# The gate's sixteen modulation tiles by quarters inside the up projection, and a transformer block's end in a written order

## The chip, the cores and the metric

The kernel runs on one core of one Trainium2 chip. The metric is the device time of one execution in microseconds (us), the median of several runs; lower is better. The core has five engines with a queue of their own, which run side by side and wait for each other through semaphores: TensorE (PE, matmuls), VectorE (DVE), ScalarE (ACT), GpSimd (POOL) and SyncE (SP, which here only issues transfers). Every instruction of one engine runs in the order of that engine's queue. Transfers (DMA) move data between the device memory and the on-chip memory.

## The reference

One block of a diffusion transformer over 512 latent tokens, with 256 context tokens beside them; the model width is 2048, the feed-forward width 5504, all in 32-bit floats. What matters for the change:

```python
mod_l = (jax.nn.silu(c) @ w_ada[l] + b_ada[l])[:, None, :]
sh_a, sc_a, gt_a, sh_f, sc_f, gt_f = jnp.split(mod_l, 6, axis=-1)
...
x = x + gt_a * merge_heads(att_l, conv_l, g_mix_out[l], w_out[l])
...
hf_l = modulate(rms_norm(x, g_ffn_norm[l]), sh_f, sc_f)
x = x + gt_f * conv_ffn(hf_l, w_up[l], ffn_conv_w[l], ffn_conv_b[l], w_down[l])
return rms_norm(x, g_final)
```

`mod_l` has 6 x 2048 = 96 x 128 values. The kernel keeps them as 96 columns of 128 (a *modulation tile* each): 32 to 47 are `gt_a`, 48 to 63 `sh_f`, 64 to 79 `sc_f`, and 80 to 95 `gt_f`, the gate of the feed-forward part, which is first needed when the down projection's second sum is scaled.

## The kernel before

**Precision.** A matmul in 32-bit precision is made of three (`mm3`, lines 183 to 185): each operand is split into a high and a low part, and high x high, high x low and low x high are summed. For a weight tile ACT writes the high part (a CAST, line 984) and DVE the low part (line 985). So for every product PE waits for ACT first, and one matmul later for DVE.

**Stages.** The input projection runs to 430 us of the profiled execution, the attention to 625, the output projection to 808. There the residual, the norm of its result and the modulated input `hf` of the feed-forward part are made. The up projection begins with plain rows (tiles `uf`, weights `ufw0`, `ufw1`, ...). From 880 to 1680 us it runs over f = 3 to 42 by seven products per f, in the manner of Strassen and Winograd: `p1`, `p2`, `p6`, `q5`, `p7`, and one f later `q4` and `q3`. A product (`product`, line 1151) is 24 matmuls of 128 x 256. Its operands are four weight tiles and sums of them: of the loads `11`, `12`, `s1`, `s3` and `22` that SP issues (line 1105), `s1` and `s3` are added to in memory by a POOL transfer (line 1107), then DVE computes a11 += s1 (line 1199) and a12 += a11 (line 1200). The five tiles take their place in a ring of nine buffers, so a load of f+2 starts when a product of f is done with its tile. The down projection follows: 7 plain rows to 1782 us, then 24 steps v0 to v23 of the same seven products, with 18 matmuls each, to 2141 us. Its results are the tiles c0 to c15 (`into`, line 1312). Step v22 yields c12 and c13, v23 c14 and c15.

**Modulation tiles.** A tile is a dot product of a row block of `w_ada` with silu(c): a load of 128 x 2048 values and DVE's multiply-and-sum. Tiles 32 to 87 are done in the output projection, in halves of 1024 (`late_dot`, line 247, DVE line 251, tiles `ada`). Tiles 88 to 95 are done by quarters of 512 (`gate_mods`, line 1227, DVE line 1234, tiles `aq`) in the plain rows of the down projection.

**Between the projections.** The last two tiles of the output projection are computed in halves of 256 tokens (`ol`). For the first half, then for the second, DVE adds the residual (line 943, tiles `x14`, `x15`), ACT squares it, DVE adds the squares up (line 335, `fq0t`), PE sums over partitions (line 300), ACT takes the root (line 277, with a table load), DVE the reciprocal (line 279, `rr`), PE spreads it over the partitions (line 284), and `hf_tile` (line 919) multiplies, scales and splits each tile (`x0`, `hf0h`, `hf0l`, ...).

**The end.** The final norm goes by halves of 256 tokens too. `scale_out` (line 1390) scales c tiles by the gain on ACT into `out` tiles (line 1393), `final` (line 1381) multiplies by the reciprocal root on DVE (line 1386) and issues the stores (line 1387). The last two steps and the end are written out from line 1437 on.

**Order.** The program order is written by hand only in part: a scheduler with a cost table of its own reorders each engine's instructions ahead of the run. `keep` fixes an instruction's place among those kept, `tc.issue_after` sets one behind another, and generators (`pump`, `next(gm)`) deal out side work between products: `pump(1)` takes one step of the list `bg`, which holds above all the pair sums of the convolution (`pair_sums`, tiles `ts`, `tp`).

## Time and profile before

| | |
|---|---|
| median of 3 runs | 2158.14 us |
| the three runs | 2158.14, 2150.28, 2158.75 us |
| the profiled execution | 2158.0 us |
| its span (first to last instruction) | 2156.2 us |
| outside of the span | 1.8 us |
| mean granted TensorE clock | 0.992 |
| idle time of PE in the span | 2156.2 - 2104.1 = 52.1 us |

The span is what the views of the profile divide up. A busy PE is not always at its peak: the profile gives beside the busy time the clock that was granted, 1.00 being full. The views used below are the page's table of engines, the windows (a row for a stretch: its length, each engine's busy time with its instructions, the granted clock, the share of time in which the transfer engines were busy, and GB/s), the list of what PE waited for (tile and line that waited, the releaser, total us, times, and longest), and the timeline (start in us, duration in us, engine, line, operation, output <- inputs, and in brackets the idle time ahead with what ended it). The timeline leaves the buffers' numbers out of the names: `v` is any of a step's weight tiles, `v23s` its `s1` or `s3`, `u_s` those of the up projection, `c` any c tile.

### The profile page before, as it was taken

Reading aid. Unit: us, or ns where it says so; the run is one execution under the profiler, and the core shown is the slowest. Engines: PE = TensorE matmul, PEld = TensorE weight load, DVE = VectorE, ACT = ScalarE, POOL = GpSimd, SP = SyncE. Lnnn points to the kernel's source line nnn. Section 1 sums busy time; section 2 is a strip of 40 time slices with the busy share of each in tenths; the row PEclk is TensorE's granted clock in tenths of the full one; section 3 lists DMA queues with packets and bytes.
Section 4 is the critical chain, followed back from the end, with each engine's and each line's share of the span. In section 5 each row is a group of like instructions: output and inputs, shape, how many; then the busy total and the mean of one; then the engine's idle time right before and its main releaser. Section 6 shows DMA issues by size and latency. Waiting matters only on the chain.

```text
span 2156.2 us, 37750 instructions
## 1 busy us (share of the span) xinstructions
PE 2104.1 (98%) x14458; PEld 1946.8 (90%) x14458; DVE 1770.6 (82%) x2859; ACT 1046.8 (49%) x1709; POOL 188.1 (9%) x270
## 2 busy tenths in 40 slices
PE   7999999999999999999999999999999999999996
PEld 4788788888988888999999999999999889999996
DVE  7998987778886989788888888788888659888886
ACT  5533333555542237555555555555555333333445
POOL 0000000000000000111111111111111000000000
PEclk9999999999999999999999999999999999999998
DMA  9989885334559986677877877887877998877773
GB/s 338 348 274 334 268 284 177 130 125 157 181 198 345 357 272 187 160 216 201 242 230 215 239 225 223 239 235 214 238 229 219 345 331 289 260 217 235 210 234 110
DMA packets 162409, 513.89 MB, mean 238 GB/s; under 512 B 18994, under 2 KB 23346, under 8 KB 156594
## 3 DMA queue, kind: packets, MB, share of 16 engines
q1 hardware_dynamic: 132564, 417.10, 56.7%
q0 software_dynamic: 27488, 92.29, 18.2%
q8 instruction: 113, 1.85, 0.3%
q10 hardware_dynamic: 2176, 2.10, 0.3%
q14 instruction: 68, 0.56, 0.1%
HBM read 464.22 MB, written 46.14 MB: 237 GB/s over the span
## 4 chain that ended last, share of the span: by engine, by line
PE 90%; DVE 4%; DMA 3%; ACT 2%; issue 1%; SPq 0%; DVEq 0%; ACTq 0%
PE pp L183 4%; PE pp L185 4%; PE pp L184 4%; PE o L183 1%; PE o L184 1%; PE o L185 1%; PE d L183 1%; PE d L185 1%; PE d L184 1%; PE uf L183 1%; DMA ada<-in_w_ada 1%; PE uf L184 1%; PE uf L185 1%; PE of L183 1%; PE of L184 1%; PE of L185 1%
## 5 line engine op out<-in xcount | busy, mean ns | idle before, releaser
L1030 POOL DMA_DIRECT2D t_d<-tp x126 | 71.8, 573 | 469.1 <-DVE tp L1029 466.7
L251 DVE SCALAR_TENSOR_TENSOR ada<-ada,sv 128x1024 f32<-128x1024 f32 x68 | 82.1, 1220 | 13.5 <-DMA ada<-in_w_ada 13.5
L166 ACT CAST w_0h<-rw 128x512 fp32r<-128x512 f32 (+1 forms) x63 | 38.3, 618 | 106.2 <-PE pp L184 65.4
L1107 POOL DMA_DIRECT2D u_s<-in_w_up x80 | 70.2, 877 | 225.2 <-DMA u_s<-in_w_up 109.8
L229 DVE SCALAR_TENSOR_TENSOR ada<-ada,sv 128x1024 f32<-128x1024 f32 x64 | 77.6, 1219 | 3.8 <-DMA ada<-in_w_ada 3.6
L510 DVE SCALAR_TENSOR_TENSOR ada<-ada,svc 128x1024 f32<-128x1024 f32 x64 | 76.0, 1220 | 2.8 <-DMA ada<-in_w_ada 2.8
L1028 ACT CAST tp<-a 128x256 fp32r<-128x256 f32 x90 | 34.7, 404 | 63.2 <-DMA t_d<-tp 51.8
L773 POOL TENSOR_TENSOR gr<-gr,half 128x8 f32<-128x8 f32 x4 | 10.1, 2522 | 627.8 <-DVE gr L772 535.8
L167 DVE TENSOR_TENSOR w_0l<-rw,w_0h 128x512 fp32r<-128x512 f32 (+1 forms) x63 | 42.6, 682 | 21.7 <-ACT w_0h L166 21.7
L251 DVE SCALAR_TENSOR_TENSOR ra<-ra,sv 128x1024 f32<-128x1024 f32 x44 | 52.5, 1219 | 1.4 <-DMA ra<-in_w_ada 1.3
L1199 DVE TENSOR_TENSOR u<-u,u_s 128x1024 f32<-128x1024 f32 x40 | 48.8, 1220 | 1.1 <-DMA u_s<-in_w_up 1.0
L1200 DVE TENSOR_TENSOR u<-u,u 128x1024 f32<-128x1024 f32 x40 | 48.7, 1218 | 0.0
L1029 DVE TENSOR_TENSOR tp<-a,tp 128x256 fp32r<-128x256 f32 x90 | 36.2, 418 | 13.8 <-ACT tp L1028 13.7
L744 ACT CAST pth<-t 128x384 fp32r<-128x384 f32 x64 | 28.6, 485 | 26.5 <-PE t L741 26.5
L521 DVE TENSOR_TENSOR acc<-acc,pp 128x512 f32<-128x512 f32 x50 | 34.0, 681 | 2.1 <-PE pp L185 2.1
L745 DVE TENSOR_TENSOR ptl<-t,pth 128x384 fp32r<-128x384 f32 x64 | 33.3, 550 | 2.7 <-ACT pth L744 2.7
L1028 ACT CAST tp<-ts 128x256 fp32r<-128x256 f32 x36 | 14.6, 407 | 41.5 <-DMA t_d<-tp 39.6
L725 DVE TENSOR_REDUCE mn<-s 128x1 f32<-128x768 f32 x32 | 30.4, 953 | 4.7 <-PE s L714 4.6
L1029 DVE TENSOR_TENSOR tp<-ts,tp 128x256 fp32r<-128x256 f32 x36 | 15.2, 422 | 22.3 <-ACT tp L1028 22.3
L991 ACT ACTIVATE g<-cg,sm 128x512 f32<-128x512 f32 x40 | 32.5, 813 | 0.6 <-DVE cg L1168 0.6
L991 ACT ACTIVATE a<-ca,sm 128x512 f32<-128x512 f32 x40 | 32.1, 803 | 0.0
L999 ACT ACTIVATE g<-g 128x512 f32<-128x512 f32 x43 | 27.1, 631 | 6.4 <-DVE g L993 6.4
(15965 smaller groups left out, 9401.3 us busy)
## 6 DMA issues: line engine op xcount, KB each, us to landing
ada<-in_w_ada SPq DMA_DIRECT2D x196, 512.0 KB, 6.0
u<-in_w_up SPq DMA_DIRECT2D x120, 512.0 KB, 8.3
w<-t_d SPq DMA_DIRECT2D x161, 256.0 KB, 5.3
u_s<-in_w_up SPq DMA_DIRECT2D x80, 512.0 KB, 4.2
u_s<-in_w_up POOLq DMA_DIRECT2D x80, 512.0 KB, 9.1
t_d<-tp POOLq DMA_DIRECT2D x126, 256.0 KB, 4.9
v<-in_w_dnw SPq DMA_DIRECT2D x72, 384.0 KB, 5.4
ra<-in_w_ada SPq DMA_DIRECT2D x22, 1024.0 KB, 4.9
```

Of the source, the lines that this page charges most:

```text
L183: PE.matmul(ps, w[0], x[0], start=first, stop=False, skip_group_check=on_top)
L184: PE.matmul(ps, w[0], x[1], start=False, stop=False, skip_group_check=on_top)
L185: PE.matmul(ps, w[1], x[0], start=False, stop=last, skip_group_check=on_top)
L229: V.scalar_tensor_tensor(out=r, in0=r, scalar=1.0, in1=vec[:, i * 1024:(i + 1) * 1024], op0=ALU.mult, op1=ALU.mult, accum_out=col[:, i:i + 1])
L251: keep(V.scalar_tensor_tensor(out=r, in0=r, scalar=1.0, in1=svs[i], op0=ALU.mult, op1=ALU.mult, accum_out=lc[:, t % 4:t % 4 + 1] if i else ...
L510: keep(V.scalar_tensor_tensor(out=raw[q], in0=raw[q], scalar=1.0, in1=svc[:, q * 1024:(q + 1) * 1024], op0=ALU.mult, op1=ALU.mult, accum_o ...
L991: A.activation(u, src, AF.Identity, bias=s("fb", m), scale=s("fw", 86 + m))
L1028: A.copy(out=z[:, :256], in_=src)
L1029: V.tensor_tensor(out=z[:, 256:], in0=src, in1=z[:, :256].bitcast(F32), op=ALU.subtract)
L1030: G_.dma_start(t_d[p, OPS.index(n)], z.bitcast(F32))
L1107: G_.dma_start(r[-1], src[more], accum_op=ALU.add)
L1199: V.tensor_tensor(out=a11, in0=a11, in1=s1, op=ALU.add)
```

## The change

It has four parts.

1. Of the tiles 80 to 95, eight leave the output projection (`late["end"]` goes from 88 to 80) and eight leave the plain rows of the down projection. All sixteen are now done as 64 quarters inside the up projection's products: `between` takes a step of `bg`, or, when `bg` is empty, the next quarter. A quarter is one 256 KB load into the single buffer `ts`, which the pair sums use too, and one DVE multiply-and-sum of 128 x 512; the next load can start when that buffer is free.
2. The tiles `12` and `s3` of the last step get buffers of their own rather than two of the ring.
3. The first matmuls behind a norm's sums and behind its spread are issued after them (`hold`, `behind`), at the end of the down projection.
4. The end's order is written out: the table for the root is loaded ahead by a small root of its own, `pump` sits inside products, the c tiles' last sums and the output products are kept in the order written, and the first half's stores are all issued by SP.

```diff
-    late = {"t": 32, "raw": None, "end": 88}
+    late = {"t": 32, "raw": None, "end": 80}
...
     def mm3(ps, w, x, first, last, on_top=False):
-        PE.matmul(ps, w[0], x[0], start=first, stop=False, skip_group_check=on_top)
+        with tc.issue_after(behind.pop()) if behind else ExitStack():
+            PE.matmul(ps, w[0], x[0], start=first, stop=False, skip_group_check=on_top)
...
+    def gate_mods():
+
+        for q in range(4):
+            SP.dma_start(rl, sv_d[:, q * T:(q + 1) * T])
+            for i in range(16):
+                r = cp.tile([P, T], F32, tag="ts", bufs=1, name=f"aq{i}{q}")
+                SP.dma_start(r, w_ada[80 + i][:, q * T:(q + 1) * T])
+                yield
+                V.scalar_tensor_tensor(out=r, in0=r, scalar=1.0, in1=rl, op0=ALU.mult, op1=ALU.mult, accum_out=parts[q // 2][:, i, q % 2:q % 2 + 1])
...
+    def between():
+
+        if bg:
+            pump(1)
+        else:
+            next(gm, None)
+
     def product(ps, a, n, nm, first):
...
-        pump(1)
+        between()
...
-        z.a11, z.s1, z.a12, z.s3, z.a22 = (raw4(f"v{st}{x}")[:, :n] for x in ("11", "s1", "12", "s3", "22"))
+        own = ("12", "s3") if st == STEPS - 1 else ()
+        z.a11, z.s1, z.a12, z.s3, z.a22 = ((dp.tile([P, 2 * T], F32, tag="sq", bufs=2, name=f"v{st}{x}") if x in own else raw4(f"v{st}{x}"))[:, :n] for x in ("11", "s1", "12", "s3", "22"))
...
-            (A if j % 4 else SP).dma_start(out[j:j + 2, :, HS[h]].rearrange("a p t -> p a t"), o)
+            (A if h and j % 4 else SP).dma_start(out[j:j + 2, :, HS[h]].rearrange("a p t -> p a t"), o)
...
-    bg.append(rms_steps(sqs, D, 0, T // 2, rl, wait=1, one=True))
+    bg.append(rms_steps(sqs, D, 0, T // 2, rl, wait=1, one=True, hold=True))
     outs = final(0, rl[:, HS[0]], scaled)
-    d_q5(za)
+    with tc.issue_after(last_hi[0]):
+        A.activation(tiny(1, "root"), eps, AF.Sqrt)
+    pump(1)
+    d_q5(za, (3,))
     squares(za.m + 1, H1)
-    pump(2)
-    d_q5(zb)
+    d_q5(zb, (1,), lambda: [keep(next(outs)) for _ in range(2)])
+    keep(last_into[0])
     squares(zb.m + 1, H1)
-    pump(1)
     scaled = {j: scale_out(j, 1) for j in range(0, za.m, 2)}
-    for _ in range(3):
-        next(outs)
+    keep(next(outs))
     d_q3(za)
+    keep(last_into[0])
     sqs = [ssq, add_squares(None, acc2[za.m][:, H1], T // 2, "eqc", a=T // 2)]
-    for _ in range(3):
-        next(outs)
+    for _ in range(2):
+        keep(next(outs))
     d_q3(zb)
+    keep(last_into[0])
+    for _ in range(2):
+        keep(next(outs))
     sqs.append(add_squares(None, acc2[zb.m][:, H1], T // 2, "eqd", a=T // 2))
     *_, r = rms_steps(sqs, D, T // 2, T // 2, None, one=True)
+    keep(recips[0])
     for ins in outs:
         keep(ins)
```

How this moves the instructions shows at three places. The first is DVE's queue at the end of the output projection; `x14` and `x15` are the last two residual tiles by halves, `fq0t` the sum of squares, `ada86` and `ada87` modulation tiles. Before:

```order
L251 SCALAR_TENSOR_TENSOR ada860_7370,mod_90<-ada860_7370,sv_93 128x1024
L943 SCALAR_TENSOR_TENSOR x14_7265<-ol0_7263,mod_90,x14_7265 128x256
L251 SCALAR_TENSOR_TENSOR ada861_7372,lc_94<-ada861_7372,sv_93 128x1024
L251 SCALAR_TENSOR_TENSOR ada870_7408,mod_90<-ada870_7408,sv_93 128x1024
L335 TENSOR_TENSOR fq0t_6497<-fq0t_6497,fq14_7508 128x256
L279 RECIPROCAL rr_7488<-rr_7488 128x2
L251 SCALAR_TENSOR_TENSOR ada871_7410,lc_94<-ada871_7410,sv_93 128x1024
L256 TENSOR_TENSOR mod_90<-mod_90,lc_94 128x4
L257 TENSOR_TENSOR mod_90<-mod_90,sm_82 128x4
L943 SCALAR_TENSOR_TENSOR x15_7267<-ol1_7264,mod_90,x15_7267 128x256
```

And now:

```order
L283 RECIPROCAL rr_7436<-rr_7436 128x2
L955 SCALAR_TENSOR_TENSOR x14_7243<-ol0_7241,mod_90,x14_7243 128x256
L347 TENSOR_TENSOR fq0t_6497<-fq0t_6497,fq14_7456 128x256
L938 TENSOR_TENSOR x0_6494<-x0_6494,rl_92 128x256
L938 TENSOR_TENSOR x1_6500<-x1_6500,rl_92 128x256
...
L942 TENSOR_TENSOR hf0l_7496<-x0_6494,hf0h_7495 128x256
L938 TENSOR_TENSOR x2_6507<-x2_6507,rl_92 128x256
L942 TENSOR_TENSOR hf1l_7520<-x1_6500,hf1h_7519 128x256
L938 TENSOR_TENSOR x3_6514<-x3_6514,rl_92 128x256
L274 SCALAR_TENSOR_TENSOR fs4_7876<-mod_90,sm_82 128x1
L955 SCALAR_TENSOR_TENSOR x15_7245<-ol1_7242,mod_90,x15_7245 128x256
```

The dots ahead of the last residual are gone, the reciprocal of the first half stands ahead of `x14`, and the first `hf` tiles are made ahead of `x15`.

The second place is the up projection. SP's queue, around the loads of f = 13 and 14 (`aq101` is quarter 1 of tile 80 + 10):

```order
L1119 DMA u13_11_10613<-in_w_up 128x1024
L1119 DMA u13_12_10615<-in_w_up 128x1024
L1175 DMA aq101_10430<-in_w_ada 128x512
L1175 DMA aq111_10464<-in_w_ada 128x512
L1119 DMA u13_s1_10617<-in_w_up 128x1024
L1119 DMA u13_s3_10620<-in_w_up 128x1024
L1175 DMA aq121_10496<-in_w_ada 128x512
L1119 DMA u13_22_10623<-in_w_up 128x1024
L1119 DMA u14_11_10872<-in_w_up 128x1024
```

Before, the same loads of `11`, `12`, `s1`, `s3`, `22` followed one another with nothing between them. The quarters' loads now stand ahead of `s1` and between `s3` and `22`, each waiting for the one buffer `ts`. On DVE the multiply-and-sum of `aq101` stands between a12 += a11 of f = 12 and the low part `u11q4l`, that of `aq111` behind `u11q3l`, and that of `aq121` ahead of `u12p7l`; quarters are found so up to f = 28.

The third place is DVE's queue in the last two steps. Before, from the second product of v22 on:

```order
L985 TENSOR_TENSOR v22p2l_23364<-v2212_23131,v22p2h_23363 128x768
...
L985 TENSOR_TENSOR v22p6l_23465<-v2211_23129,v22p6h_23464 128x768
L1319 SCALAR_TENSOR_TENSOR c14_19136<-v23a_23413,mod_90,c14_19136 128x256
L1273 TENSOR_TENSOR v23s3_23329<-v2311_23326,v23s1_23327 128x768
...
L985 TENSOR_TENSOR v21q3l_23488<-v2112_22934,v21q3h_23487 128x768
L1319 SCALAR_TENSOR_TENSOR c12_19132<-v22a_23337,mod_90,c12_19132 128x256
L1329 TENSOR_TENSOR v2311_23326<-v2311_23326,v23s1_23327 128x768
L1330 TENSOR_TENSOR v2312_23328<-v2312_23328,v2311_23326 128x768
```

And now:

```order
L999 TENSOR_TENSOR v22p2l_23405<-v2212_23172,v22p2h_23404 128x768
L1296 TENSOR_TENSOR v23s3_23370<-v2311_23367,v23s1_23368 128x768
...
L999 TENSOR_TENSOR v23p2l_23481<-v2312_23369,v23p2h_23480 128x768
L1342 SCALAR_TENSOR_TENSOR c12_19187<-v22b_23379,mod_90,c12_19187 128x256
L1355 TENSOR_TENSOR v2311_23367<-v2311_23367,v23s1_23368 128x768
L1342 SCALAR_TENSOR_TENSOR c11_19185<-v21a_23181,gn_95,c11_19185 128x256
L999 TENSOR_TENSOR v22p6l_23506<-v2211_23170,v22p6h_23505 128x768
L1356 TENSOR_TENSOR v2312_23369<-v2312_23369,v2311_23367 128x768
```

The sum `s3` = a11 + s1 of v23, behind which POOL adds to `s1` in memory, now stands right behind `v22p2l`, and a11 += s1, which needs that addition, six rows ahead of `v21q3l` rather than two behind it. On ACT the high part `v23p6h`, made from that a11, stands behind 11 output scalings rather than 15, counted from `v21q3h`.

More of the change, by code (lines that the diff above doesn't have):

```diff
@@ L299, in rms_steps @@
             for g in range(ng):
-                PE.matmul(ps[:, g:g + 1], sq[:, a + g * P:a + (g + 1) * P], ones[:, 0:1], start=i == 0 and g == 0, stop=i == len(sqs) - 1 and g == ng - 1)
+                ins = PE.matmul(ps[:, g:g + 1], sq[:, a + g * P:a + (g + 1) * P], ones[:, 0:1], start=i == 0 and g == 0, stop=i == len(sqs) - 1 and g == ng - 1)
+        if hold:
+            behind.append(ins.ins)
         r = tiny(4, "rr")[:, :ng]
@@ L304, in rms_steps @@
             yield
-        spread(pb, r)
+        ins = spread(pb, r)
+        if hold:
+            behind.append(ins)
         if dst is not None:
@@ L1214, in block_kernel @@
     finish(pend)
+    assert next(gm, None) is None
     phc.close()
@@ L1290, in block_kernel @@
             pump(1)
-            for _ in range(2):
-                next(gm, None)
             for _ in range(2 if h == 0 else 3):
@@ L1410, in block_kernel @@
         d_q5(z)
-        next(gm, None)
         if first:
```

60 lines of the change are left out of this document (29 added, 31 removed).

## The prediction

> **What bounds the kernel now.** The page's table of engines comes first, then windows over the long stages.
>
> ```profile
> span 2156.2 us, 37750 instructions
> PE 2104.1 (98%) x14458; PEld 1946.8 (90%) x14458; DVE 1770.6 (82%) x2859; ACT 1046.8 (49%) x1709; POOL 188.1 (9%) x270
> ...
> 625.00:808.00 183.00, 183.00 (x886) 152.97 (x885) 150.01 (x275) 56.73 (x99) 11.97 (x18) 0.99 0.90 324
> 880.00:1680.00 800.00, 800.00 (x6653) 799.25 (x6653) 663.27 (x877) 461.52 (x689) 139.62 (x208) 1.00 0.79 224
> 1680.00:1782.00 102.00, 100.99 (x529) 86.00 (x528) 60.19 (x115) 36.64 (x53) 6.05 (x10) 1.00 0.96 343
> ```
>
> PE is busy for 2104.1 of 2156.2 us, and in the output projection (625 to 808) and the up projection (880 to 1680) it has no idle time. The clock there is 0.99 to 1.00. So work taken from DVE or the transfers inside those stages gains nothing; only PE's few gaps can. The list of PE's waits says where those are:
>
> ```profile
> PE v23a L183 <- ACT v23p6h L984: 3.6, 1, 3.6
> PE rs L300 <- DVE fq0t L335: 3.0, 1, 3.0
> PE rs L300 <- ACT eqdt L331: 2.2, 1, 2.2
> ```
>
> The change touches three of these places: the boundary (`fq0t`, `ufw0h`), the last two steps (`v23p6h`) and the end (`eqdt`). The windows there also show a lower clock:
>
> ```profile
> 810.00:815.00 5.00, 2.48 (x13) 2.40 (x13) 4.50 (x14) 4.38 (x10) 0.54 (x1) 0.74 0.99 322
> 815.00:820.00 5.00, 5.00 (x28) 5.00 (x28) 4.47 (x11) 4.32 (x11) 0.00 (x0) 0.58 1.03 413
> 820.00:825.00 5.00, 5.00 (x45) 5.00 (x44) 4.69 (x16) 4.09 (x12) 0.00 (x0) 1.00 0.97 383
> 2095.00:2100.00 5.00, 4.27 (x36) 4.06 (x35) 4.26 (x7) 2.61 (x4) 0.00 (x0) 1.00 0.40 157
> 2120.00:2125.00 5.00, 5.00 (x32) 5.00 (x32) 3.48 (x7) 2.72 (x5) 0.00 (x0) 0.69 0.00 0
> ```
>
> Behind each of the two long gaps PE is busy without a break, but at 0.58 and 0.69 of its clock: 28 and 32 instructions in 5 us, where 45 fit at a full clock in the row from 820. That is (45 - 28) x 0.111 = 1.9 us lost in 815 to 820 alone, and with the parts of the neighbouring slices some 2.8 us behind each gap. A gap costs its length and then this.
>
> **The change, part by part.** *The boundary.* The timeline of before:
>
> ```profile
> 807.80 0.28 PE L185 MATMUL ol<-mx15h,o151w1536l 128*128 128x256 f32 x1
> 808.56 1.23 DVE L251 SCALAR_TENSOR_TENSOR ada<-ada,sv 128x1024 f32<-128x1024 f32 x1 [0.36 <-DMA ada<-in_w_ada]
> 810.11 0.48 DVE L943 SCALAR_TENSOR_TENSOR x<-ol,mod,x 128x256 f32<-128x256 f32 x1
> 811.17 0.42 DVE L335 TENSOR_TENSOR fq0t<-fq0t,fq 128x256 f32<-128x256 f32 x1
> 811.64 0.61 PE L300 MATMUL rs<-io,fq0t 128*128 128x1 f32 x4 [2.96 <-DVE fq0t L335]
> 812.25 0.83 ACT L984 CAST ufw0h<-ufr 128x768 fp32r<-128x768 f32 x1
> 813.13 0.58 PE L183 MATMUL uf<-hf0h,ufw0h 128*128 128x256 f32 x1 [0.88 <-ACT ufw0h L984]
> ```
>
> PE's last dense matmul ends at 808.08. The residual that follows from it (810.11) stands behind a dot (808.56) that waited for its load, and starts 2.0 us late. Without the dots: the residual from about 808.2 (0.48), the square 0.4, the sum 0.42, and PE's sums at about 809.7. ACT, meanwhile, has one scaling of 0.4 and then `ufw0h` (0.83) behind the square, so the plain rows start at about 809.2 + 0.4 + 0.4 + 0.83 + 0.1 = 811.0 rather than 813.13: **2.1 us** gained. At worst ten DVE operations that now stand ahead of `x15` are late by as much (0); at best the restart follows PE's sums at once, 2.1 + 0.8 = 2.9. Whether the lower clock stays is taken up below.
>
> *The last two steps.*
>
> ```profile
> 2097.01 0.95 DVE L985 TENSOR_TENSOR v22p2l<-v,v22p2h 128x768 fp32r<-128x768 f32 x1
> ...
> 2103.55 0.48 DVE L1319 SCALAR_TENSOR_TENSOR c<-v21a,gn,c 128x256 f32<-128x256 f32 x1 [0.60 <-PE v21a L185]
> ...
> 2104.63 0.84 ACT L984 CAST v23p2h<-v 128x768 fp32r<-128x768 f32 x1 [4.89 <-DMA v<-in_w_dnw]
> 2109.12 0.85 POOL L1274 DMA_DIRECT2D v23s<-in_w_dnw  x1 [20.20 <-DVE v23s L1273]
> 2110.04 6.09 ACT L1393 ACTIVATE out<-c,sm 128x256 f32<-128x256 f32 x15
> 2114.19 0.96 DVE L1329 TENSOR_TENSOR v<-v,v23s 128x768 f32<-128x768 f32 x1 [2.67 <-DMA v23s<-in_w_dnw]
> 2116.91 0.58 PE L183 MATMUL v23a<-w,v23p6h 128*128 128x256 f32 x1 [3.57 <-ACT v23p6h L984]
> ```
>
> The chain is: `s3` on DVE, POOL's addition into `s1`, which lands 2114.19 - 2109.97 = 4.2 us after POOL is done, a11 += s1, and `v23p6h` on ACT behind 15 scalings of 6.09 / 15 = 0.41 us. Now `s3` follows `v22p2l` (2097.01), so POOL's addition can be issued near 2100 and land at about 2104, and ACT becomes the last. Its wait of 4.89 us for `v23p2h`'s load goes, since that load now has a buffer of its own; the next high part then starts when PE frees its buffer, behind the product that ended at about 2103.4 (the row of 2103.55), where it started at 2104.63 + 0.74 = 2105.4. The rest of ACT's queue comes 1.9 earlier with it: the scalings from 2108.1, 11 of them 4.5, `v23p6h` 0.8: ready at 2113.4. PE's products ahead of it, which ended 3.6 before 2116.9 at 2113.3, lose smaller waits and end at about 2112. PE restarts at 2113.5 and waits once more, 0.8, for the low part: in effect 2114.4 rather than 2116.9, less 0.3, because the `s3` put in ahead pushes back `v21q4l`: **2.2 us** gained. With no second wait it is 3.0. If POOL's addition takes 9.2 us to land, as in the up projection (1289.91 to 1299.08, below), a11 += s1 comes at 2109 and holds up the low part of `v22p6` behind it by 3, and 0.5 or so is left.
>
> *The clock behind the gaps.* The gaps were 813.13 - 808.08 = 5.1 and 3.6 us, and are now about 2.9 (with PE's small sums in between) and 1.6 + 0.8. In 2095 to 2100 PE was idle for 0.73 at a clock of 1.00. So the trace bounds the limit: a gap of 0.7 keeps the clock, one of 3.6 loses it. Mine lie in between; the shorter, split one is nearer to the lower end. I take it that the tail's 2.8 us are won and the boundary's are not: **2.8 us**, between 0 and 5.6. [...]
>
> *The end.*
>
> ```profile
> 2139.26 3.69 DVE L1386 TENSOR_TENSOR out<-out,rl 128x512 f32<-128x512 f32 x6
> 2142.87 0.48 DVE L1319 SCALAR_TENSOR_TENSOR c<-v23c,mod,c 128x256 f32<-128x256 f32 x1
> 2145.36 1.27 DVE L1386 TENSOR_TENSOR out<-out,rl 128x512 f32<-128x512 f32 x2
> ```
>
> The last sum into c14 (2142.87) stands behind six output products of 3.69 / 6 = 0.61 us. Now two products, a sum of squares and one product stand there, with two of the six put behind: from 2139.3 that is 2 x 0.61 + 0.42 + 0.61 = 2141.5, 1.4 earlier, and PE's wait of 2.2 for `eqdt`, the square of c14, falls by as much. Between the reciprocal and the second half's products stands one product, not two: 0.6 earlier. **2.0 us**, from 0 (the spread of the root ends last) to 3.0 (the five saved products in full).
>
> *The up projection* takes the 64 quarters. Their cost on DVE is in the rows of before, and so is what stands near it:
>
> ```profile
> L1234 DVE SCALAR_TENSOR_TENSOR aq<-aq,svq x32: 683/687/693, 1703.2 to 1788.1; 128x512 f32<-128x512 f32 x32
> ...
> 1285.55 3.60 SPq L1105 DMA_DIRECT2D u_s<-in_w_up  x2
> ...
> 1289.91 0.89 POOL L1107 DMA_DIRECT2D u_s<-in_w_up  x1 [1.23 <-DMA u_s<-in_w_up]
> ...
> 1299.08 1.23 DVE L1199 TENSOR_TENSOR u<-u,u_s 128x1024 f32<-128x1024 f32 x1 [0.18 <-DMA u_s<-in_w_up]
> 1300.82 1.22 DVE L985 TENSOR_TENSOR u24p2l<-u,u24p2h 128x1024 fp32r<-128x1024 f32 x1
> 1303.76 1.22 DVE L985 TENSOR_TENSOR u23q4l<-u,u23q4h 128x1024 fp32r<-128x1024 f32 x1
> 1304.48 0.29 PE L185 MATMUL u24b<-hf1h,u24p2l 128*128 128x256 f32 x1
> ...
> 1305.01 2.47 SPq L1105 DMA_DIRECT2D u_s<-in_w_up  x2
> ...
> 1299.00:1301.00 2.00, 2.00 (x19) 2.00 (x18) 1.93 (x3) 0.62 (x1) 0.00 (x0) 1.00 1.06 274
> 1303.00:1305.00 2.00, 2.00 (x19) 2.00 (x18) 2.00 (x3) 1.23 (x4) 0.00 (x0) 1.00 0.04 14
> ```
>
> 64 x 0.69 = 44 us of DVE go beside 800 - 663 = 137 us of idle DVE. But there is a loop: `u23q4l` ends at 1304.98 and frees the buffer for the next `s1` load (issued 1305.01; the one before 1285.55); load 4.4, POOL's addition 9.2, then a11 += s1, `p2l` and `q4l` again, 5.9: 19.5 us, against PE's 20 us per f. PE needs `u24p2l`, ready at 1302.04, at 1304.48: 2.4 us in hand. A quarter's load is 256 KB, at the 274 GB/s of a full stretch 0.95 us; one in three falls into the idle transfers of 1303 to 1305 (0.04), the others share with load and addition. With some three quarters in an f the loop grows to 19.5 + 0.5 to 1.2; a dot ahead of `q4l` (0.6) stands where a piece of the convolution (0.4 to 0.7) stood. That is 20.0 to 20.7, over 22 f with quarters and less the 2.4 in hand: 0 to 13 us lost. Nearest to the row with 0.18 of waiting is the low end; I take **1.5 us**.
>
> *The down projection's start* loses 32 dots and loads. PE has 101.0 of 102 us there: at most 1.0, taken as 0. The same holds for the output projection (183.00 of 183). The table load on ACT and the stores moved to SP cost nothing beside a waiting PE.
>
> **The sum**, against the profiled execution (2158.0, which is 0.1 under the median): 2158.0 - 2.1 - 2.2 - 2.8 - 2.0 + 1.5 = **2150.4 us**.
>
> **The rivals.** *Both gaps keep the clock*: 2.8 more, 2147.6. For it: the boundary's new gap is broken by PE's sums. Against: 2.9 is close to the 3.6 that lost it. [...] *Neither does*: 2153.2. *The quarters eat the gain*: the loop at 20.3 gives 22 x 0.3 = 7 less 2.4 in hand, and further waits of a quarter for its own load, up to about 6 in all; 2155 to 2158, no change. *Slower*: the loop at 21.2 us or more, when two quarters of 0.95 each prolong both load and addition in full and a dot adds 0.6 to DVE's part. Each f then takes the loop's time: 22 x 1.2 - 2.4 = 24, and 2150.4 - 1.5 + 24 = 2173. It decides from a loop of 20.5 (22 x 0.5 - 2.4 = 8.6, all of the gain). For it: transfers are full from 1290 to 1301, the loop lacks only 0.5, and the single buffer lets no load run ahead. [...] Against: 4 us in each f are all but idle, and a loop that lags starts its loads into a longer idle stretch.
>
> **How the numbers follow.** The forecast has 0.35, both clocks 0.21, neither 0.14, gain eaten 0.20, slower 0.10. Within 0.5% of 2158.1, about what a measurement of this kernel can tell from no change, is 2147.3 to 2168.9. Faster: half of *both clocks* and a little of the forecast with the upper bounds of boundary and end, 0.18. Slower: 0.09. Same: 0.73. The range runs from 2144 (both clocks and 3.6 of the bounds) to 2160; what lies beyond is most of *slower* and a tenth of the fast side.
>
> **What would show it.** The first plain row at about 811 and the slices 810 to 820 (still below 1.00); `v23p6h` awaited for under 2 us and 2110 to 2125 at a full clock; c14 behind one output product. PE in 880 to 1680 must stay at 20.0 us per f with no wait; the row to look at is a11 += s1 and its wait for `u_s`. The forecast is wrong if that wait exceeds 2 us in many f.

## The result, and the profile after

The changed kernel takes 2262.67 us (median of 4 runs, 2257.75 to 2265.75), the kernel before beside it 2158.44 (4 runs, 2150.28 to 2161.53): a ratio of **1.048 [1.046, 1.051]**. It is slower by 104 us, where 8 us faster was forecast, and outside the range of 2144 to 2160.

The head of the profile's page, its table of engines and the chain that ended last:

```profile
span 2262.9 us, 37775 instructions
PE 2136.8 (94%) x14458; PEld 1969.9 (87%) x14458; DVE 1772.3 (78%) x2888; ACT 1046.0 (46%) x1710; POOL 187.8 (8%) x270
...
PE 60%; DMA 21%; DVE 10%; issue 4%; ACT 3%; POOL 1%; DVEq 0%; SPq 0%; POOLq 0%; ACTq 0%
```

The work is what it was: DVE is busy 1.7 us longer than before, ACT 0.8 less. What is new are 126.1 us in which PE stands, 52.1 before, and a chain that leaves PE for transfers and DVE in 31 of 100 parts, 7 before. The windows say where (columns as before the prediction: length; busy us and instructions of PE, PEld, DVE, ACT, POOL; granted clock; transfer share; GB/s):

```profile
880.00:1280.00 400.00, 373.12 (x3002) 368.86 (x3002) 316.27 (x453) 202.04 (x290) 53.46 (x77) 0.97 0.77 219
1280.00:1680.00 400.00, 353.69 (x2784) 349.38 (x2783) 295.59 (x434) 194.54 (x303) 68.96 (x105) 0.94 0.73 210
```

The up projection, without a gap before, has 73 us of idle PE in these 800, and behind the gaps a clock of 0.97 and 0.94. The transfers are not busier than before (0.77 and 0.73), and DVE and ACT are less so. So no engine is the bound: they wait for each other. From the end of f = 3 to the end of f = 42 (the last matmul of `p7`, read from the timeline) the stage takes 897.4 us against 786.0: **111.4 us**, more than the whole loss. PE stands for 77.1 us of it; the other 34 go with the lower clock behind the gaps, so a gap costs its length and then more, as the prediction has it for the boundary. The list of waits (who waited, line, for whom: total us, times, longest us):

```profile
PE u24a L187 <- ACT u24p1h L998: 7.4, 1, 7.4
PE u31a L187 <- ACT u31p1h L998: 5.2, 1, 5.2
...
PE u7a L189 <- DVE u7p1l L999: 3.9, 1, 3.9
...
DVE tp L1043 <- ACT tp L1042: 84.5, 34, 7.9
DVE aq L1177 <- DMA aq<-in_w_ada: 71.0, 30, 6.6
...
DVE u L1242 <- DMA u_s<-in_w_up: 4.8, 3, 2.7
...
ACT tp L1042 <- DMA t_d<-tp: 142.5, 47, 10.2
```

PE waits for high parts that ACT makes late (47 of the 77 us, 35 of them at `p1h`) and for low parts that DVE makes late (30, of them 18 at `p1l`). DVE waits 71 us for quarters' own loads; the row that was to be watched, a11 += s1 for `u_s`, has 4.8. And ACT waits up to 10.2 us at a cast of the pair sums (`tp`) for the store of an earlier `tp` tile. Of before the same row reads:

```profile
ACT tp L1028 <- DMA t_d<-tp: 91.4, 59, 3.5
```

So ACT always waited there, often, and it cost PE nothing; what is new is the longest. The timeline around PE's wait of 7.4 us (start, duration, engine; in brackets the idle time ahead and what ended it):

```profile
1338.41 1.03 ACT L998 CAST u23p7h<-u_s 128x1024 fp32r<-128x1024 f32 x1
1338.43 0.84 POOL L1121 DMA_DIRECT2D u_s<-in_w_up  x1 [0.78 <-DMA u_s<-in_w_up]
1338.97 0.87 POOL L1044 DMA_DIRECT2D t_d<-tp  x1
1340.77 0.58 POOL L1044 DMA_DIRECT2D t_d<-tp  x1 [0.93 <-DVE a L1007]
...
1349.66 0.40 ACT L1042 CAST tp<-a 128x256 fp32r<-128x256 f32 x1 [10.22 <-DMA t_d<-tp]
1349.98 1.04 ACT L998 CAST u24p1h<-u 128x1024 fp32r<-128x1024 f32 x1
1350.10 0.42 DVE L1043 TENSOR_TENSOR tp<-a,tp 128x256 fp32r<-128x256 f32 x1 [7.92 <-ACT tp L1042]
1351.07 0.58 PE L187 MATMUL u24a<-hf0h,u24p1h 128*128 128x256 f32 x1 [7.43 <-ACT u24p1h L998]
```

ACT stands at a `tp` cast for a store to land. Behind it in ACT's queue stands `u24p1h`, which waited for nothing itself; DVE stands at the cast's other half, and PE at `u24p1h`. Two such casts had run at 1335.09 and 1335.55, and the third, next of the sums, finds its tile still held by a store, which POOL issued at 1338.97 and which took 10.7 us to land. A landing of that length is nothing new: the 126 stores took 4.9 us in the median and 11.7 at the longest before, 5.1 and 12.0 after. New is where the casts that wait for them stand. Counted in the trace, three casts start within 4 us 11 times after the change, twice before it.

The order of the program shows why they come in clumps. DVE's queue at f = 10 to 12, `ts1` and `tp1..` being pair 1 of the sums; before the change, then after (rows left out at "..."):

```
L985 TENSOR_TENSOR u11p2l<-u11_12,u11p2h 128x1024
L1034 TENSOR_TENSOR ts1<-a9 128x256
L985 TENSOR_TENSOR u10q4l<-u10_22,u10q4h 128x1024
...
L985 TENSOR_TENSOR u12p2l<-u12_12,u12p2h 128x1024
L1042 SCALAR_TENSOR_TENSOR ts1<-ts1,a10 128x256
```

```
L1043 TENSOR_TENSOR tp111<-a9,tp111 128x256
L999 TENSOR_TENSOR u10q3l<-u10_12,u10q3h 128x1024
L1177 SCALAR_TENSOR_TENSOR aq81,modc_91<-aq81,rl_92 128x512
...
L1177 SCALAR_TENSOR_TENSOR aq121,modc_91<-aq121,rl_92 128x512
L999 TENSOR_TENSOR u12p7l<-u12_s3,u12p7h 128x1024
L1048 TENSOR_TENSOR ts1<-a9 128x256
L1056 SCALAR_TENSOR_TENSOR ts1<-ts1,a10 128x256
```

The two steps of `ts1` were seven products apart; now the single buffer goes to five quarters first; the first step comes twelve products later than it did, the second five, and both together. At f = 24 the sums are at pair 5 where they were at 7; they make it up in a hurry until f = 36. So 38 of the 111 us are lost in f = 29 to 42, behind the last quarter (at 1452.6 us, in f = 28).

### The profile page after: what moved, and what is told of

Its sections match the earlier page's. It is cut to its first block, busy times and chain, and to the rows that moved or that the text cites. A ratio compares the mean times of both kernels' runs of the same rounds, so it can differ in the third digit from the quotient of the medians.

```text
span 2262.9 us, 37775 instructions
## 1 busy us (share of the span) xinstructions
PE 2136.8 (94%) x14458; PEld 1969.9 (87%) x14458; DVE 1772.3 (78%) x2888; ACT 1046.0 (46%) x1710; POOL 187.8 (8%) x270
## 4 chain that ended last, share of the span: by engine, by line
PE 60%; DMA 21%; DVE 10%; issue 4%; ACT 3%; POOL 1%; DVEq 0%; SPq 0%; POOLq 0%; ACTq 0%
DMA t_d<-tp 7%; DMA aq<-in_w_ada 7%; DMA u_s<-in_w_up 4%; PE pp L187 4%; PE pp L189 4%; PE pp L188 4%; PE o L187 1%; PE o L189 1%; PE o L188 1%; DMA ada<-in_w_ada 1%; PE d L187 1%; PE d L188 1%; PE d L189 1%; PE of L187 1%; PE of L188 1%
## 5 line engine op out<-in xcount | busy, mean ns | idle before, releaser
L1044 POOL DMA_DIRECT2D t_d<-tp x126 | 77.4, 631 | 433.7 <-DVE tp L1043 410.2
L1177 DVE SCALAR_TENSOR_TENSOR aq<-aq,rl 128x512 f32<-128x512 f32 x64 | 44.1, 688 | 71.2 <-DMA aq<-in_w_ada 71.0
L233 DVE SCALAR_TENSOR_TENSOR ada<-ada,sv 128x1024 f32<-128x1024 f32 x64 | 77.6, 1219 | 3.9 <-DMA ada<-in_w_ada 3.7
L255 DVE SCALAR_TENSOR_TENSOR ada<-ada,sv 128x1024 f32<-128x1024 f32 x52 | 62.7, 1219 | 8.0 <-DMA ada<-in_w_ada 7.9
L1042 ACT CAST tp<-ts 128x256 fp32r<-128x256 f32 x36 | 14.6, 405 | 58.7 <-DMA t_d<-tp 38.9
L1005 ACT ACTIVATE g<-cg,sm 128x512 f32<-128x512 f32 x40 | 32.6, 814 | 7.6 <-DVE cg L1211 5.4
```

Source lines behind the costliest of these rows:

```text
L233: V.scalar_tensor_tensor(out=r, in0=r, scalar=1.0, in1=vec[:, i * 1024:(i + 1) * 1024], op0=ALU.mult, op1=ALU.mult, accum_out=col[:, i:i + 1])
L255: keep(V.scalar_tensor_tensor(out=r, in0=r, scalar=1.0, in1=svs[i], op0=ALU.mult, op1=ALU.mult, accum_out=lc[:, t % 4:t % 4 + 1] if i else ...
L1042: A.copy(out=z[:, :256], in_=src)
L1044: G_.dma_start(t_d[p, OPS.index(n)], z.bitcast(F32))
```

## The experiments

Suspected were: the buffer `ts` that quarters and pair sums share (theory A); a dot in DVE's queue that waits for its own load (B); the transfers themselves, on the loop of the `s1` loads (C, the prediction's rival); the dots as such, which take DVE's time and put other work late in the queues (D); and a special form of that (E): a cast of the sums right ahead of `p1h`. "Stretch" is the time from the end of `p7` of f = 3 to that of f = 42 in the profiled run, "idle" the part of it in which PE stands. Each ratio is to the kernel before as it ran beside that kernel (medians 2156.84 to 2160.20). Where PE has no gap the stretch repeats: 786.0 us in four kernels, and 785.2 in e1.

| kernel | median us | ratio [95%] | stretch | idle |
|---|---|---|---|---|
| before | 2158.44 | 1 | 786.0 | 0 |
| after | 2262.67 | 1.048 [1.046, 1.051] | 897.4 | 77.1 |
| e1 no quarters there, the rest of the change | 2157.48 | 0.999 [0.997, 1.000] | 785.2 | 0 |
| e2 sums with tiles of their own | 2209.87 | 1.024 [1.020, 1.027] | 845.0 | 44.5 |
| e3 quarters in a ring, one load ahead | 2212.96 | 1.024 [1.021, 1.028] | 851.8 | 46.5 |
| e4 shared buffer, no loads | 2203.58 | 1.021 [1.017, 1.024] | 840.9 | 38.9 |
| e5 own tiles, no loads | 2169.80 | 1.005 [1.003, 1.007] | 803.6 | 15.5 |
| e6 own tiles, a quarter per 4 products | 2161.11 | 1.001 [0.999, 1.003] | 796.6 | 12.6 |
| e7 own tiles, behind each p1 and p7 | 2210.10 | 1.024 [1.021, 1.027] | 846.8 | 41.5 |
| e8 no quarters anywhere | 2147.17 | 0.994 [0.992, 0.996] | 786.0 | 0 |
| e9 e6 without loads | 2157.97 | 1.000 [0.999, 1.002] | 795.6 | 12.7 |
| e10 all 64 in the down projection | 2161.30 | 1.002 [1.000, 1.003] | 786.0 | 0 |
| e11 shared buffer, loads without dots | 2219.97 | 1.029 [1.026, 1.033] | 857.7 | 52.1 |
| e12 own tiles, 32 quarters, one per f | 2153.63 | 0.998 [0.997, 0.999] | 786.0 | 0 |
| e13 the same, at another product | 2142.96 | 0.993 [0.990, 0.996] | 783.2 | 1.2 |
| e14 e12 with the buffer shared | 2210.65 | 1.024 [1.020, 1.028] | 844.2 | 32.6 |

**Is it the quarters' place at all?** e1 and e8 keep the ends of the change. In e1, tiles 80 to 87 are back in the output projection and 88 to 95 in the down projection's plain rows; e8 has no quarters.

```diff
-    late = {"t": 32, "raw": None, "end": 80}
+    late = {"t": 32, "raw": None, "end": 88}
...
-        between()
+        pump(1)
```

> Without the quarters in the up projection: tiles 80 to 87 go back to the output projection, 88 to 95 to the down projection (their quarters of silu(c) are loaded one at a time), the last step's own buffers and the written end stay. All theories put the whole loss into the up projection, so they agree: PE has no idle time from 880 to 1680 us, the last steps gain 4.1 and the end 2.3 us as in the changed kernel, about 2152 us. Above 2156 would say that the end gives nothing.

```diff
-        for q in range(4):
+        for q in range(0):
...
-        for z in parts:
+        for z in ():
```

> The changed kernel without the quarters, their loads and dots (the gate is not the reference's); nothing is put back into the output projection or the down projection. The order of the up projection is that of before. All theories: the forecast's terms without the loss, boundary 2 to 5 us, last steps 4, end 2, so 2147 to 2151 us. Above 2155 would mean that the boundary gives nothing.

Both bring the up projection back to 786 (785.2, 786.0): all 111 us hang on the quarters in it. e8 says what the other parts are worth without any quarter: 11 us. e1 was to take about 2152 us and took 2157.48. That isn't because the end gives nothing: the last two steps and the end take 59.3 and 27.8 us rather than 61.75 and 29.65. It loses 2.7 us in the steps v0 to v19, and with the dots back in the output projection PE's gap at the boundary is 6.4 us, 5.0 before.

**The shared buffer.** e2 gives each pair sum a tile of the ring of five:

```diff
-        t = tmp([P, T], F32, f"ts{p}") if p == PAIRS - 1 else cp.tile([P, T], F32, tag="ts", bufs=1, name=f"ts{p}")
+        t = tmp([P, T], F32, f"ts{p}")
```

> As the changed kernel, but the pair sums take their tile from the ring of five and no longer share the quarters' single buffer. In the scheduled order the pair sums then keep the places that they had before (pair 7 at f = 24, where the changed kernel is at pair 5), and each quarter still waits for its own load with one buffer. Theory A (the shared buffer delays the pair sums, which then come in clumps and block ACT and DVE): the loss goes, 2148 to 2160 us. Theory B (dots stand in DVE's queue and wait for their own load, 71 us in all): waits of 1 to 2.4 us for most of the 64 quarters stay, 2190 to 2250 us. Theory C (17 MB more of transfers delay the loop of s1 loads): 2190 to 2250 us as well.

That wins 52 of 111 us, so theory A holds, but not alone: it had forecast the whole. The sums' order is again that of before (pair 7 at f = 24), and almost nothing is lost once the quarters are done, at f = 22. What is left stands in its list of waits:

```profile
PE u20a L187 <- ACT u20p1h L998: 4.9, 1, 4.9
...
DVE aq L1177 <- DMA aq<-in_w_ada: 46.6, 19, 6.6
```

e3 leaves the sums' buffer alone and takes the quarters out of it, into the same ring, with a load issued one dot ahead:

```diff
-                r = cp.tile([P, T], F32, tag="ts", bufs=1, name=f"aq{i}{q}")
+                r = tmp([P, T], F32, f"aq{i}{q}")
                 SP.dma_start(r, w_ada[80 + i][:, q * T:(q + 1) * T])
+                todo.append((q, i, r))
                 yield
...
+                if len(todo) == 2:
+                    dot()
```

> As the changed kernel, but the quarters take their tiles from the ring of five, and each load is issued one quarter ahead of its dot. The pair sums have the shared buffer alone. Neither sharing nor waiting for a load in DVE's queue: theories A and B say 2147 to 2158 us. Theory C (the transfers themselves) says over 2190 us, since the same bytes move in the same stage.

Another way to part them, with the like gain (46 us). One load ahead did not take the rest away, though A and B said so; by this expectation C would be right, and e9 below speaks against it. Two things are in the trace. DVE still waits 36.4 us for quarters' loads (46.6 in e2). And 29 of the 66 us that are left are lost from f = 24 on, with no quarter in the stage any more: nine times, in every second f, a cast of the sums stands straight ahead of `p1h` on ACT and waits 3.4 to 4.5 us for a store. In before no cast stands there.

**Loads or dots?** e4 leaves out the loads, e5 also gives the sums tiles of their own, and e11 keeps the loads in the shared buffer but not the dots.

```diff
-                SP.dma_start(r, w_ada[80 + i][:, q * T:(q + 1) * T])
                 yield
-                V.scalar_tensor_tensor(out=r, in0=r, scalar=1.0, in1=rl, ...
+                V.scalar_tensor_tensor(out=r, in0=rl, scalar=1.0, in1=rl, ...
```

> As the changed kernel without the quarters' loads (the dots multiply the quarter of silu(c) by itself, so the gate is not the reference's). The dots' DVE time (44 us) and the shared buffer stay. If dots on DVE by themselves cost: over 2165 us. Theories A, B and C all need a load that is waited for or that takes transfer time: 2147 to 2155 us.

> As e4 (all 64 dots, no loads, so the gate is not the reference's), but the pair sums take their tile from the ring of five, and in the scheduled order they then stand on ACT as before, but for one of seven; as in e2 behind the last quarter, where no time was lost. Theory D (44 us more of DVE in themselves stop PE): 2195 to 2205 us, as e4. Theory E (a cast of the pair sums stands on ACT straight ahead of the high part of p1 and waits for a store, which e4 shows up to f = 40, long behind the last dot): 2146 to 2158 us.

```diff
-                V.scalar_tensor_tensor(out=r, in0=r, scalar=1.0, in1=rl, ...
...
+            V.tensor_copy(out=z, in_=s("b_ada", 64, 32).rearrange("p (i q) -> p i q", q=2))
```

> The changed kernel with the quarters' loads into the shared buffer but without the dots (the gate is the bias alone). Theory C (transfers): a large part of the 110 us stays, over 2190 us. Theory B (waits on DVE for a quarter's load) with E (pair sums displaced): little of it stays, since no instruction on DVE waits for a load and the pair sums are displaced up to f = 27 only: 2150 to 2180 us.

Without any added transfer, the shared buffer and the dots still cost 55 us (e4), where A, B and C had forecast no loss; 33 of them are lost from f = 24 on, behind the last dot, at casts that wait ahead of `p1h` as in e3. With transfers and without dots 72 are lost (e11), which is what its expectation gives to theory C. But there the sums' own first step waits for the quarter's load that has the buffer, and in four cases the profile names a load of `u_s` or `u`, issued by SP too:

```profile
DVE ts L1048 <- DMA aq<-in_w_ada: 21.8, 3, 8.5
DVE ts L1048 <- DMA u_s<-in_w_up: 15.3, 2, 10.0
DVE ts L1048 <- DMA u<-in_w_up: 12.0, 2, 9.1
```

With neither (e5), 18 us are left, all from f = 6 to 15; 2169.80 us is neither the 2195 to 2205 of theory D nor the 2146 to 2158 of E. So three costs can be told apart, though they don't add up exactly: the shared buffer (111 to 59), dots that wait for their loads (59 to 18), and the dots themselves. The last step is not clean: without loads to wait for, the dots of e5 come closer together and are done at 1106 us, those of e2 at 1334.

**The place of the dots.** e6 pins each dot behind the low part of every fourth product, with tiles of their own for the sums; e7 behind those of `p1` and `p7`; e9 is e6 without loads, in the same order.

```diff
+        last_lo[:] = [V.tensor_tensor(out=lo[:, :n], ...).ins]
...
+                with tc.issue_after(last_lo[0]):
+                    V.scalar_tensor_tensor(out=r, in0=r, scalar=1.0, in1=rl, ...
...
-        if bg:
-            pump(1)
-        else:
+        turns[0] += 1
+        if turns[0] % 4 == 0:
             next(gm, None)
+        else:
+            pump(1)
```

> All of the change's work with its loads, the pair sums' tile from the ring of five, and each dot set behind the low part of every fourth product, from f = 3 to 39: a dot has 11 us for its load, and DVE has one dot in 11 us. On ACT the cast of the pair sums' fifth or sixth store (921 of pair 9) now stands straight ahead of u29p1h, as in e4, in every second f. Theory B (waits for a quarter's own load) and D (DVE's time): 2148 to 2160 us. Theory E: 3 to 4 us in every second f from 10 to 40, about 2195 to 2210 us.

```diff
+        if nm[-2:] in ('p1', 'p7'):
```

> As e6, but two dots in each f, behind the low parts of p1 and p7, and the pair sums step at the other five products. The casts then stand ahead of q5, q4 and p2 (two of them together) and ahead of p1 only in four f in all. Theory E: less than e6, 2150 to 2180 us. Theory B or D: 2150 to 2165 us, and no less than e6.

> e6 without the quarters' loads (the gate is not the reference's); every engine's instructions stand in the same order as in e6. e6 lost 10.6 us in the up projection, in waits of 0.6 to 3.8 us for the high part of p1 in every fourth f, behind a cast that waits for a store. If the loads' transfer time does it (theory C, through the stores' landing): the loss goes, 2147 to 2151 us. If the order alone does it (theory E): it stays, 2157 to 2161 us.

All 64 quarters evenly spread cost 10.6 us (e6); the same number behind `p1` and `p7` cost 61. In e7 every second dot (`p1`, right behind `p7`) comes only one product behind the dot that frees the buffer for its load, and DVE waits for that load (e7 was to take 2150 to 2180 us by any theory):

```profile
DVE aq L1179 <- DMA aq<-in_w_ada: 36.7, 31, 3.0
```

This wait, 28.2% of the chain from 880 to 1790 us, is what e6 hardly has (4.8 us in 7). It need not be all: in e7 a cast of the sums also stands straight ahead of `p2h` in 25 f, each time waiting 3.9 to 6.3 us for a store, and no run separates the two. For quarters that no one waits for, e9 settles theory C. Its first half beside e6's, e6 first:

```profile
880.00:1280.00 400.00, 396.24 (x3299) 394.78 (x3298) 346.78 (x493) 228.14 (x338) 68.00 (x100) 1.00 0.83 240
```

```profile
880.00:1280.00 400.00, 395.03 (x3288) 393.44 (x3287) 344.64 (x490) 227.68 (x337) 67.54 (x100) 1.00 0.77 217
```

Transfer share 0.77 rather than 0.83, and PE loses as much (9.6 against 10.6 us): 17 MB of added loads, where no one waits for them, are worth about 1 us. What costs the 10 us that both lose can be read from the traces. PE's only waits in e6 are eight, of 0.6 to 3.8 us, at `p1h` in every fourth f. The longest:

```profile
1323.16 0.40 ACT L1043 CAST tp<-a 128x256 fp32r<-128x256 f32 x1 [5.51 <-DMA t_d<-tp]
1323.47 1.04 ACT L999 CAST u25p1h<-u 128x1024 fp32r<-128x1024 f32 x1
1324.56 0.58 PE L187 MATMUL u25a<-hf0h,u25p1h 128*128 128x256 f32 x1 [3.85 <-ACT u25p1h L999]
```

In e6 a cast stands straight ahead of `p1h` in 25 f. In 17 of them it waits for nothing and PE has no gap; in eight it waits 2.3 to 5.5 us for a store, and PE waits each time 1.7 us less than the cast did. e9 has the same 25 places and eight waits of 1.4 to 3.9 us. That is theory E, though in every fourth f and not in every second as it was forecast: what costs is not that a cast stands there, but that it waits there.

**Out of the stage.** e10 puts all quarters into the down projection, two in each plain row and then one behind five of the seven products of a step (the edit of the plain rows is shown).

```diff
+            for _ in range(2):
+                next(gm, None)
```

> All of the change, with the correct gate, but the 64 quarters stand in the down projection: two in each plain row, the rest one behind each product of steps v0 to v7, from the ring of five. The order of the up projection is that of before. All theories: the gain of e8 (2147) is kept if the transfers of the plain rows (0.96 busy in before) bear 17 MB in 1700 to 1900 us: 2146 to 2151 us. If they don't, PE waits for weights in the plain rows and this gives 2155 to 2175 us.

The plain rows carry them free, but from v0 on they cost: v0 to v19 take 303.0 us rather than 284.2. The window of e10 there, beside it that of before:

```profile
1780.00:1880.00 100.00, 95.17 (x760) 92.65 (x759) 90.15 (x177) 33.86 (x42) 5.08 (x6) 0.98 0.96 315
```

```profile
1780.00:1880.00 100.00, 99.87 (x842) 99.67 (x841) 88.25 (x139) 39.32 (x47) 5.94 (x7) 1.00 0.87 269
```

Here, at a transfer share of 0.96, added quarters do have a price. Whether loads or dots make it isn't shown: PE's longest waits there are for low parts and sums of DVE (2.2 us for `v4p6l`), not for weights.

**Half and half, and the buffer again.** e12 does tiles 80 to 87 in the up projection, one quarter per f behind a fixed product, and 88 to 95 in the plain rows as before; the sums have tiles of their own. e13 differs in the product alone, e14 in the buffer alone.

```diff
+        turns[0] += 1
+        pump(1)
+        if turns[0] % 7 == 3:
+            next(um, None)
```

> All of the change with the correct gate, but the quarters divided: tiles 80 to 87 in the up projection, one quarter per f, each dot set behind the low part of p6 or so of its f, with the one buffer for the quarters alone (the pair sums' tile from the ring of five); tiles 88 to 95 in the plain rows of the down projection, as in before. In the scheduled order the pair sums' casts stand on ACT where they stood in before, but for one of seven. Theory E (order and spacing decide, not the quarters' work): no wait of PE in the up projection, 2146 to 2151 us. If 32 dots and 8 MB of loads cost by themselves what 64 cost in e6: 2152 to 2156 us.

```diff
-        if turns[0] % 7 == 3:
+        if turns[0] % 7 == 0:
```

> e12 with each dot set behind another product, p2: as many dots and loads, as far apart. In the scheduled order the cast of the pair sums' sixth store now stands straight ahead of the high part of p1 in every second f. Theory E: waits of 1 to 2 us there, 5 to 15 us in all over e12. Work alone: the same as e12 within 2 us.

```diff
-        t = tmp([P, T], F32, f"ts{p}")
+        t = tmp([P, T], F32, f"ts{p}") if p == PAIRS - 1 else cp.tile([P, T], F32, tag="ts", bufs=1, name=f"ts{p}")
```

> e12 with the buffer shared by quarters and pair sums again, as in the change. The pair sums' casts then stand in twos, ahead of p7 and of p2. Theory A (sharing is what costs most): the pair sums wait for the quarter's load and dot, 30 to 60 us over e12. If sharing is harmless at this spacing: within 5 us of e12.

The windows of e12, then of e14:

```profile
880.00:1280.00 400.00, 400.00 (x3335) 400.00 (x3334) 344.61 (x469) 230.63 (x337) 68.27 (x101) 1.00 0.82 234
1280.00:1680.00 400.00, 400.00 (x3336) 400.00 (x3335) 342.21 (x477) 231.44 (x349) 72.04 (x108) 1.00 0.83 239
```

```profile
880.00:1280.00 400.00, 385.12 (x3114) 380.89 (x3114) 318.69 (x431) 212.25 (x314) 63.00 (x93) 0.97 0.76 218
1280.00:1680.00 400.00, 382.30 (x3067) 377.53 (x3066) 320.17 (x447) 210.31 (x322) 66.76 (x100) 0.96 0.77 221
```

The same dots and the same loads, at the same place in the program: with tiles of their own PE has no gap at all in the up projection, with one shared buffer 58 us are lost, as theory A had it. (That e12 took 2153.63 us, and not the 2146 to 2151 of an up projection without waits, lies elsewhere: v0 to v19 take 288.9 us, 284.8 in e8, and the stretch behind the boundary 84.1, 82.7 in e8.) The two waits that tell it, of e14 (in e12 the second row's longest is 3.1 us):

```profile
PE u13b L187 <- ACT u13p2h L999: 3.0, 1, 3.0
...
ACT tp L1043 <- DMA t_d<-tp: 113.8, 44, 8.0
```

In e14 the sums are not a pair late (7 at f = 24, as before), but each pair is held until a quarter has left the buffer, and then comes in one piece: in DVE's order `ts1`, `ts1`, `tp11`, `tp13` stand within six rows. Three casts start within 4 us 13 times, in e12 twice, and from f = 11 to 35 every second f, one per pair, takes 21.8 to 26.8 us. e13 has the lowest median, 0.7% under before (0.5 to 1.0%) and 5% under the change; its four runs, 2140.93 to 2150.81 us, overlap those of e8 (2142.71 to 2148.92). Its PE waits in the up projection are 1.2 us in all, where theory E had 5 to 15. In its trace 17 casts stand straight ahead of `p1h`, none of which waits for a store; e12 has the same 17, so the two runs do not differ in that. One more suspicion falls here: that SP's queue, which stands at a quarter's load until the buffer is free, holds up the weights' loads behind it. From 880 to 1690 us SP stands so for 192 us after the change, but also for 179 in e13, where next to nothing is lost, and for 12 in e14, where 58 are.

## Why the prediction was wrong, point by point

**The failed step is the up projection's term**, "I take 1.5 us", with its bounds of 0 to 13; it measured 111.4. It priced a quarter as 0.69 us of DVE and 0.95 us of transfers on the loop of the `s1` loads, and the rival *slower* was that loop again. That loop was not what decided: a11 += s1 waited 4.8 us in all, the transfer share did not rise, and e9 and e12 carry 17 and 8 MB of loads at 1 us and none. The prediction did name "the single buffer", but only as a reason that no load runs ahead of its dot. That the pair sums use the buffer too was written down ahead of it; in the sum this stands at nothing, without a reason. Yet the sums need it: their steps then wait for a quarter's load and dot, come late and in clumps, and their casts stand waiting in ACT's queue ahead of the high parts that PE waits for. e2 against after (52 us) and e14 against e12 (58) show the price of sharing by one line of code each; that it goes by way of the casts is read from the traces. The second part, a dot that waits for its load at the head of DVE's queue, was mentioned as "further waits of a quarter for its own load, up to about 6 in all": DVE waited 71 us for them after the change, and removing the loads from e2 (e5) wins 41. The sign that the prediction had named for being wrong, a wait of a11 += s1 above 2 us in many f, did not show, and it was wrong all the same. (Its loop is set against 20 us per f where before has 20.16; that only makes the term smaller.)

The sentence on cover, that 44 us of DVE "go beside 800 - 663 = 137 us of idle DVE", was true and no help: idle time that lies behind a wait in the same queue wasn't free here, where DVE stood 71 us at the quarters' loads and 84.5 at casts of the sums. That a quarter prolongs the `s1` load and POOL's addition, from which the loop and the rival *slower* take their bounds, was the author's estimate. In the up projection it hardly shows: from 880 to 1460 us of the changed kernel `s1` and `s3` landed 4.2 us behind the issue of their load and 9.4 behind that of the addition (medians; 4.3 and 9.1 before), and e6, at a transfer share of 0.83, lost 1 us more than e9 at 0.77. e10's window at 0.96 would fit a price of the transfers, though DVE's dots are added there too.

**The other terms held in the main.** *The boundary*, forecast 2.1: PE's gap fell from 5.04 to 2.60 us, 2.4 gained. *The clock behind it* was taken as not won; in this run it was. The windows after:

```profile
810.00:815.00 5.00, 3.00 (x25) 2.72 (x24) 3.78 (x12) 4.55 (x9) 0.54 (x1) 1.00 0.89 271
815.00:820.00 5.00, 5.00 (x45) 5.00 (x44) 5.00 (x11) 3.40 (x10) 0.00 (x0) 1.00 0.99 332
```

45 instructions in 815 to 820 at a full clock, 28 before. But the same gap went otherwise in other runs (last section), where four of fourteen profiled runs lost it, so that this one kept it is luck.

*The last two steps*, forecast 2.2 and 2.8 for the clock. The waits shrank as forecast, in each row:

```profile
2210.63 0.95 DVE L1296 TENSOR_TENSOR v23s<-v,v23s 128x768 f32<-128x768 f32 x1
2212.11 0.85 POOL L1297 DMA_DIRECT2D v23s<-in_w_dnw  x1 [10.24 <-ACT v21q4h L998]
2212.85 0.83 ACT L998 CAST v23p2h<-v 128x768 fp32r<-128x768 f32 x1 [0.36 <-PE v22b L188]
2226.52 0.39 PE L187 MATMUL v23a<-w,v23p6h 128*128 128x256 f32 x1 [1.58 <-ACT v23p6h L998]
```

`v23p2h` waits 0.36 us rather than 4.89, POOL's addition is issued as `v22p2` ends rather than 9 us behind it, and PE waits 1.58 rather than 3.57. From the end of v19 to that of `v23p7` it was 60.40 us against 61.75, so 1.4 of the 5.0; in e1 to e14 it was 57.4 to 59.6, so 2.2 to 4.4. Part of the lower clock stayed:

```profile
2225.00:2230.00 5.00, 2.99 (x18) 2.78 (x19) 2.81 (x4) 5.00 (x11) 0.00 (x0) 0.88 0.00 0
2230.00:2235.00 5.00, 5.00 (x36) 5.00 (x36) 4.58 (x9) 4.84 (x10) 0.00 (x0) 0.78 0.00 0
```

and PE waited 0.9 us each for the low parts `v19q4l`, `v20q4l` and `v21q4l`, which the sum did not have (0.7 for `v21q4l` before).

*The end*, forecast 2.0, gave 2.3: 27.39 us from `v23p7` to the end, 29.65 before. The last sum into c14 now starts 0.1 us behind PE's last matmul, 1.9 before (2142.87 and 2140.96):

```profile
2249.71 0.69 DVE L1413 TENSOR_TENSOR out<-out,rl 128x512 f32<-128x512 f32 x1
2250.32 0.48 DVE L1342 SCALAR_TENSOR_TENSOR c<-v23c,mod,c 128x256 f32<-128x256 f32 x1
```

*The output and the down projection* were put at 0 and stayed there (v0 to v19: 284.3 against 284.2; the output projection ended 2.9 us later in the profiled run, within the 806.1 to 813.9 that the profiled runs of the experiments show for it). With the failed term at 0, as in e8, the forecast's sum would be 2148.9; e8 has 2147.2. In part that is luck: in e8's profiled run the boundary's gap gives 2.4, the clock behind it 2.7 that the sum had at 0, the last two steps 4.2 of 5.0, and the end 2.0.

## What to carry to other kernels

Here a buffer that two chains of side work shared made each wait for the other (58 us between e12 and e14), and the scheduler, which honours it, moved whole groups of instructions: ask of every tile that a change reuses who else holds it and for how long, and look in the order not only for the instruction put in but for how far the others moved, whether they now stand in clumps, and which of them will stand waiting straight ahead of work that the main engine needs. With PE waiting on two in-order queues, the price of side work was set by what it stood waiting for at the head of a queue, not by its busy time: the same 64 quarters, 44 us of DVE, cost 10.6 us in e6 and 61 in e7. Give it a tile of its own, issue its load well ahead of its use, and pin it at even distances. Here 32 quarters cost nothing in the up projection that way (e12); all 64 still cost 10 us (e6), and no run has them free.

## What the runs showed of the hardware that was not expected

One and the same gap of 2.60 us at the boundary, in which PE stands for 2.0 us around its small sums, costs nothing or up to 2.8 us, by the execution. The stretch behind it, to the end of `p7` of f = 3, took 82.7 to 82.8 us in nine profiled runs (e3 to e5, e7 to e11, e14), 84.0 and 84.1 in e13 and e12, and 85.5 in e6, each time without a wait of PE; where it is longer, the first 5 us have a lower clock (0.50 to 0.71; the slices from 810 and 815 us have 0.86 and 0.80 in e13, and 1.00 twice in e8). In e2 (85.8, first 5 us at 0.66) and in the changed kernel (84.1, at a full clock) waits of 1.2 and 1.0 us for `u3q5h` are in it. The windows of e6:

```profile
810.00:815.00 5.00, 3.14 (x16) 2.85 (x15) 3.93 (x10) 4.59 (x10) 0.54 (x1) 0.72 0.94 326
815.00:820.00 5.00, 5.00 (x29) 5.00 (x29) 4.52 (x11) 3.06 (x8) 0.00 (x0) 0.60 1.01 312
```

The gap lies between the 0.7 us that kept the clock before and the 3.6 that lost it. Behind it the clock was lower in four of these runs and kept in the others; what decides, no run shows.

An up projection in which PE never waits takes 20.16 us per f, before, in e8 and in e12. Behind stalls it can take 19.94: in e13 from f = 9 to 28, behind waits of 0.6 and 0.4 us in f = 7, until it falls back to 20.16 behind one of 0.2 us. So a PE without a gap can lose 0.22 us per f that no view names; e13's 2.8 us come from it. A stall is not needed: in e1, where PE has no gap in the whole stretch, f = 40 and 41 take 19.94 too. What changes the pace stays open.
